# Longer rows for the general, rounded-weight and residual tiles of a two-layer decoder trunk, and one raw weight buffer fewer

## The chip, the cores and the metric

The kernel runs on 1 core of one Trainium2 chip. The metric is the device time of one execution in microseconds; the time before is the median of 3 runs, 2338.2 us (2337.09 to 2348.92).

## The reference

256 tokens of 2048 features go through two layers. Each layer has a token mixer and a channel mixer, and each of these is wrapped in the same way; everything is float32.

```python
mod = c_act @ ada_w[i] + ada_b[i]
sh1, sc1, g1, sh2, sc2, g2 = jnp.split(mod[:, None, :], 6, axis=-1)
h = x * (1.0 + sc1) + sh1
y = fox_attention(h, ...) if i % 2 == 0 else swa_attention(h, ...)
x = layer_norm(ALPHA * x + (1.0 + g1) * y, ln_mix_g[i], ln_mix_b[i])
h = x * (1.0 + sc2) + sh2
y = conv_ffn(h, ffn_w_up[i], ffn_conv_w[i], ffn_conv_b[i], ffn_w_down[i])
x = layer_norm(ALPHA * x + (1.0 + g2) * y, ln_ffn_g[i], ln_ffn_b[i])
```

The mixers are a softmax attention with a forget gate (16 heads of 128) in layer 0 and a sliding-window attention with sinks (32 query heads of 64, 4 key heads) in layer 1. The channel mixer is `(silu(conv(h @ w_up)) gated) @ w_down` with 2 x 5632 hidden features. All weights, about 590 MB of them, are read once.

## The kernel before, in words

**Weights as two halves.** `stream` (L254) takes 512 columns of a weight matrix and goes along its rows two chunks of 128 at a time. For each such pair a raw weight tile `w` (128 x 1024 float32, 512 KB, pool `wp`, 10 buffers) is loaded on the SP queue (L259). ScalarE rounds it into a tile `wh` (L262), and VectorE writes the rest, `w - wh`, into a tile `wl` (L273). Both lie in pool `hl`, 4 buffers for each name, used in turn. The activations are held in the same way as a rounded part and a rest, and every product is three matmuls in the rounded format: rounded by rounded, rounded by rest, rest by rounded. One helper (`mm`, L75) records all matmuls, so they are told apart by their tiles.

**Two forms of product.** In both a matmul has a *moving* operand, whose columns stream through, and a *stationary* one of 128 columns, which is loaded just before (PEld in the profile).

- `w_mm` (L306, `ws` in the profile): the weights are stationary, and 256 columns (tokens) of the modulated input `hH` or `hL` move. One pair of chunks gives 24 matmuls in a row that use one `wh` and one `wl`. It makes q and k of the first attention and the up-projections of both channel mixers: 9984 matmuls in all.
- `x_mm` (L282, `xs`): 128 tokens of the activation are stationary, and 512 columns of `wh` or `wl` move. One pair of chunks gives 12 matmuls, three for each chunk and token block. The stationary tile is `hH`/`hL` (v of the first attention, all inputs of the second, and the last four chunks of the output projections: 1056 matmuls), an attention output `oT` (576) or a gated hidden tile `gT` (2112).

**Where the tiles lie.** Pools are laid one behind the other along each partition: constants (among them `x`, `hH`, `hL`), then `wp`, `hl`, `gp`, `tp`, `sp`. `gp` has 24 general tiles of 2048 bytes (`gtile`, L59: queries, keys, v, probabilities, `oT`, `gT`). The built kernel has these first bytes in a partition:

| tile | before | after |
|---|---|---|
| `hH`, `hL` | 40640, 57024 | the same |
| `w` (10 / 9 buffers, 4096 bytes each) | 92576 and on | 92576 and on |
| `wh` (4 buffers) | 133536, 137632, 141728, 145824 | 129440, 133632, 137824, 142016 |
| `wl` (4 buffers) | 149920, 154016, 158112, 162208 | 146208, 150400, 154592, 158784 |
| first `gp` tile, and the step to the next | 166304, 2048 | 162976, 2144 |

**What sets the order.** Beside the streamed weights other work is spread by hand: the six conditioning vectors per layer (`ada_vector`) read their own 512 KB tiles (`wa`, also from `wp`, also on SP) and are multiplied on VectorE (L388); attention heads, evacuations and norms go on by one stage at each weight pair (`later`, `defer`, `step`). The DMA of a raw tile is issued on SP in program order as soon as the last reader of the buffer's previous tile is done, so a raw tile's load starts when the tile ten before it in `wp` is released. The opening reads the first conditioning vectors through the same pool as `wo` tiles (L508).

Of the kernel before, what the change touches and what calls it, by code (L numbers as in the profile page):

```python
# [11 lines left out]
F32R = mybir.dt.float32r  # L12
# [5 lines left out]
P = 128  # L18
D = 2048
S = 256  # L20
# [16 lines left out]
WB = 512  # L37
UK = 4


@with_exitstack
def hybrid_trunk(ctx: ExitStack, tc: tile.TileContext, a: dict, out: bass.AP):
# [5 lines left out]
    cst = ctx.enter_context(tc.tile_pool(name="cst", bufs=1))  # L48
    wp = ctx.enter_context(tc.tile_pool(name="wp", bufs=10))
    hl = ctx.enter_context(tc.tile_pool(name="hl", bufs=4))  # L50
# [8 lines left out]
    def gtile(name="g"):  # L59
        return gp.tile([P, 2, S], F32R, tag="g", name=name)  # L60

# [15 lines left out]
    def pin(ins, on=True):  # L77
        """Keeps ins behind what its engine has been given so far."""
        if on:
            tc.keep_in_program_order(ins)  # L80

    def split(h, l, src):
        """src (float32) -> h rounded, l the rest; the copy on ScalarE."""
        nc.scalar.copy(h, src)
        nc.vector.tensor_tensor(l, src, f32(h), op=ALU.subtract)  # L85
# [4 lines left out]

# [1 line left out]
    rows0 = ttile("rows0").rearrange("p (a b) -> p a b", b=P)  # L92
# [14 lines left out]
    nc.gpsimd.memset(m0, 0.0)  # L107
    # [:, 0]: previous block (key > query stays); [:, 1]: diagonal block (key <= query stays)
    nc.gpsimd.affine_select(out=m0[:, 0, :], in_=m0[:, 0, :], compare_op=ALU.is_gt, fill=NEG, base=0,
# [34 lines left out]
    def columns():  # L144
        """The vectors that lie along features, as columns."""
        r = ttile("rows").rearrange("p (a b) -> p a b", b=P)
# [26 lines left out]
    def rotary():  # L173
        """Sinks on every partition; sines and cosines of the positions' angles."""
        nc.gpsimd.dma_start(sink, a["swa_sinks"][0].partition_broadcast(P))
# [33 lines left out]

# [1 line left out]
    feeds, post, work = [], [], []  # L211

    def then(fn):
        """fn() behind the products of all weights streamed so far."""
        work.append(fn)
        if len(work) == 1 and not ahead[0]:
            settle()
# [9 lines left out]
    def rest(*items):  # L227
        """Residuals of the next weights."""
        n = 0
        for f in items:  # L230
            if f in residuals:
                residuals[f]()
                n += 1
            elif f in weights:
                n += 1
            if n > 2 - (items[0] not in weights):
                return
# [3 lines left out]
    def defer(gen):  # L241
        """gen goes on by one stage behind each of the next splits of weights."""
        post.append(gen)
# [10 lines left out]
    def stream(wsrc, row0, col, ks, use):  # L254
        """use(kc, h, l) for the weights [(row0 + kc) * P.., col:col+WB] of every two chunks kc, kc + 1."""
        for kc in ks[::2]:
            r0 = (row0 + kc) * P
            w = wtile()
            pin(nc.sync.dma_start(w, wsrc[r0:r0 + 2 * P, col:col + WB].rearrange("(k p) f -> p k f", p=P)), False)  # L259
            h = hl.tile([P, 2, WB], F32R, tag="wh", name="wh")  # L260
            l = hl.tile([P, 2, WB], F32R, tag="wl", name="wl")
            pin(nc.scalar.copy(h, w), False)  # L262
# [19 lines left out]
    def x_mm(ps, kc, h, l, stat, last, first=0, ts=range(NT)):  # L282
        """ps[t] [P tokens, WB] += x[:, chunks kc, kc + 1] @ w"""
        for t in ts:
            for i in range(2):
                xh, xl = stat(kc + i, t)
                mm(ps[t], xh, h[:, i, :], start=kc + i == first)
                mm(ps[t], xh, l[:, i, :])
                mm(ps[t], xl, h[:, i, :], stop=kc + i == last)

    def x_mm_end(ps, stat, nk, n):
        """Products like x_mm's; in the last weights those for the first tokens go before the others."""
        kept = []
# [12 lines left out]
    def w_mm(ps, kc, h, l, last=KC - 1, first=0):  # L306
        """ps[i] [P features, 2, S] += (x[:, chunks kc, kc + 1] @ w).T"""
        for i in range(2):
# [7 lines left out]
    def x_stationary(wsrc, col, k0, nk, stat, end=0):  # L316
        """token-major out[t] [P tokens, WB] = x @ w[:, col:col+WB]"""
        ps = x_banks()
        use = x_mm_end(ps, stat, nk, end) if end else lambda kc, h, l: x_mm(ps, kc, h, l, stat, nk - 1)
        stream(wsrc, k0, col, list(range(nk)), use)  # L320
        return ps

    def w_stationary(wsrc, col):
        """feature-major out: two banks of [P, 2, S] = (x @ w[:, col:col+WB]).T"""
        ps = w_banks()
        stream(wsrc, 0, col, list(range(KC)), lambda kc, h, l: w_mm(ps, kc, h, l))
        return ps

# [1 line left out]
    bg = {"wait": [], "run": [], "n": 0, "at": 0, "gap": 1}  # L330

    def later(gens, lag=1):
        """gens start one after another and go on by one stage at each lag-th step."""
        bg["wait"].extend((g, lag) for g in gens)
# [21 lines left out]

# [1 line left out]
    cols = {}  # L358
    gates = {}
# [67 lines left out]
    def release():  # L427
        """The columns that were kept for the time in which TensorE waits."""
        for s_, _ in held:
# [23 lines left out]

# [1 line left out]
    hH = cst.tile([P, KC, S], F32R, name="hH")  # L455
    hL = cst.tile([P, KC, S], F32R, name="hL")

    def mod_turn(k, n=1):
        """Chunks k, k + 1 of x transposed, in n banks."""
        ps = [bank() for _ in range(n)]  # L460
# [26 lines left out]
    def modulate(G, B, norm):  # L487
        """Hands the modulation of normalised x to the next weights, two chunks for each of them."""
        def feed(k):
# [8 lines left out]
    def opening(plan, proj):  # L498
        """First modulation, by pairs of chunks; between them the products that plan names for each pair."""
        CB = 2 * P  # L500
# [51 lines left out]

# [1 line left out]
    stats = cst.tile([P, NT, D // 512, nc.vector.BN_STATS_DIM], F32, name="stats")  # L554
# [25 lines left out]
    def normalise(d):  # L580
        """x <- (x - mean) / deviation, on ScalarE for the first tokens and on VectorE for the others."""
        for t in range(NT):
# [16 lines left out]
    def affine(name, l):  # L599
        """x <- ALPHA * (x * g + b)"""  # L600
        gb, bb = ln_rows(name, l)
# [13 lines left out]
    def merged(l, v, lng, lnb, ll):  # L615
        """Scale and shift of the modulation behind a layer norm with its own g and b."""
        sh, sc = cols[l, v], cols[l, v + 1]
# [6 lines left out]

# [1 line left out]
    def probs(S_ps, skc=None, nskc=None):  # L626
        """Scores [P queries, 128 | 256 keys] -> softmax."""
        regs = ((0, P), (P, 3 * P))
# [19 lines left out]
    def attend(scores, o_halves, rr, v, sinks=()):  # L648
        """The stages of one head from its scores on."""
        sps = bank("S")  # L650
# [18 lines left out]
    def o_tile(kc):  # L669
        """Where chunk kc of the attention's output goes: the last ones where the input was."""  # L670
        if kc >= KC - 4:
# [30 lines left out]

# [1 line left out]
    def fox(l, j):  # L704
# [5 lines left out]
        for b in range(4):  # L710
            nc.sync.dma_start(bfc[32 * b:32 * b + FH, :], a["fox_b_f"][j:j + 1].rearrange("l h -> h l"))
        # weights of the forget gates, in four groups of partitions of the product
        wf = wp.tile([P, KC, FH], F32, tag="w", name="wf")
# [102 lines left out]
        TC = KC // 2  # L816
        # per pair of chunks: blocks of four heads and the pairs of theirs that are multiplied then
        plan = [[], [(0, 0)], [(0, 1)], [(0, 2)], [(0, 3), (1, 0)], [(1, 1), (1, 2)], [(1, 3), (1, 4)], [(1, 5), (1, 6)], [(1, 7)]]
# [55 lines left out]

# [1 line left out]
    def rope(t, buf, nh):  # L876
        """buf [P, nh, 64], the first 16 of each head turned in place."""
        t1, t2, t3 = (tp.tile([P, SG, HR], F32, tag=n, bufs=1, name=n)[:, :nh, :] for n in ("r1", "r2", "r3"))
# [99 lines left out]

# [1 line left out]
    def conv_ffn(l):  # L980
# [63 lines left out]

# [1 line left out]
    def between(l, v, g, b, name, ll):  # L1046
        """From one layer norm, with g and b in rows g, b of lcol, to the modulated input behind it."""
        ada_need(l, v)
# [49 lines left out]
```

## Time and profile before

| | |
|---|---|
| median of the runs shown | 2338.2 us |
| lowest and highest run | 2337.09, 2348.92 us |
| span of the profiled execution | 2347.5 us |
| mean granted TensorE clock in it | 0.981 |
| read from HBM | 594.2 MB, 254 GB/s over the span |

The profiled execution is known by its span, from its first instruction to its last: 9.3 us above the median and 1.4 us below the highest run. In the profile a matmul's own duration is modelled, and matmuls overlap, so their rate is read from the distance of their starts: from the starts in the timeline, or from a piece of the chain of waits that names a length of time and a count of matmuls.

### The profile page before, as it was taken

How to read it: one execution, taken by the hardware profiler on the slowest of the kernel's cores; microseconds unless marked ns; L12 is line 12 of the kernel's file. 1: busy time of each engine (PE TensorE's matmuls, PEld its weight loads, DVE VectorE, ACT ScalarE, POOL GpSimd, SP SyncE). 2: the span in 40 equal slices, each digit the busy share in tenths (PEclk: the TensorE clock that was granted, in tenths of full speed). 3: DMA queues.
4: the chain of work that ended last, by engine and by line, in shares of the span. 5: the costliest groups of instructions: out<-in, count | busy, mean ns of one | idle time of the engine just before them, and what ended most of it. 6: DMA issues, size and time to landing. Idle time of an engine off the chain costs nothing.

```text
span 2347.5 us, 38862 instructions
## 1 busy us (share of the span) xinstructions
PE 2284.1 (97%) x15189; PEld 2075.5 (88%) x15189; DVE 1801.5 (77%) x2539; ACT 1129.1 (48%) x1677; POOL 38.4 (2%) x75
## 2 busy tenths in 40 slices
PE   6899999999999999999999999999999999999997
PEld 5799988789999888999987777789999988999986
DVE  7778878979887877887877976699877655666665
ACT  1336544445555433555534476635555543455542
POOL 1001000010000000000001000000000000000000
PEclk9899999999999999999998999999999999999999
DMA  9998989968877897887895865586878556666553
GB/s 326 304 339 270 350 313 348 332 214 310 308 248 255 294 302 262 279 291 247 289 308 196 315 209 162 165 306 216 291 258 272 180 192 194 189 189 189 189 194 112
DMA packets 285561, 598.87 MB, mean 255 GB/s; under 512 B 20790, under 2 KB 53816, under 8 KB 285376
## 3 DMA queue, kind: packets, MB, share of 16 engines
q1 hardware_dynamic: 284768, 595.85, 75.6%
q8 instruction: 119, 1.95, 0.3%
q0 software_dynamic: 608, 0.53, 0.1%
q14 instruction: 66, 0.54, 0.1%
HBM read 594.21 MB, written 2.10 MB: 254 GB/s over the span
## 4 chain that ended last, share of the span: by engine, by line
PE 92%; DVE 5%; issue 1%; DMA 1%; ACT 1%; POOL 0%; SPq 0%; DVEq 0%; ACTq 0%; POOLq 0%
PE ws L75 50%; PE xs L75 34%; PE S L75 3%; PE o L75 1%; PE sm L75 1%; DVE wl L273 1%; PE cps L75 1%; PE T L657 1%; DVE oacc L520 1%; DVE acc L388 1%; PE sm L465 1%; ACT wh L262 0%; DMA w<-in_swa_w_in_dram 0%; DMA wo<-in_ada_w_dram 0%; PE lg L75 0%
## 5 line engine op out<-in xcount | busy, mean ns | idle before, releaser
L273 DVE TENSOR_TENSOR wl<-w,wh 128x1024 fp32r<-128x1024 f32 x728 | 888.3, 1221 | 419.8 <-ACT wh L262 402.8
L262 ACT CAST wh<-w 128x1024 fp32r<-128x1024 f32 x728 | 764.3, 1052 | 907.1 <-PE ws L75 333.3
L75 PE MATMUL ws<-hH,wh 128*128 128x256 f32 x3328 | 942.1, 283 | 6.0 <-ACT wh L262 6.0
L75 PE MATMUL ws<-hH,wl 128*128 128x256 f32 x3328 | 933.7, 281 | 3.9 <-DVE wl L273 3.7
L75 PE MATMUL ws<-hL,wh 128*128 128x256 f32 x3328 | 934.6, 281 | 0.2 <-DVE hL L85 0.2
L75 PEld LDWEIGHTS ws<-hH,wh 128*128 128x128 f32 x3328 | 631.9, 190 | 10.0 <-ACT wh L262 6.8
L75 PEld LDWEIGHTS ws<-hH,wl 128*128 128x128 f32 x3328 | 630.6, 190 | 5.1 <-DVE wl L273 5.1
L75 PEld LDWEIGHTS ws<-hL,wh 128*128 128x128 f32 x3328 | 632.0, 190 | 2.7 <-issue 1.9
L75 PE MATMUL xs<-wh,gT 128*128 128x512 f32 x1408 | 437.6, 392 | 0.0
L388 DVE SCALAR_TENSOR_TENSOR acc<-wa,cact,acc 128x1024 f32<-128x1024 f32 x308 | 391.2, 1276 | 0.1
L75 PEld LDWEIGHTS xs<-wh,gT 128*128 128x128 f32 x1408 | 266.5, 189 | 55.3
L75 PE MATMUL xs<-wl,gT 128*128 128x512 f32 x704 | 275.6, 391 | 0.0
L75 PEld LDWEIGHTS xs<-wl,gT 128*128 128x128 f32 x704 | 133.2, 189 | 27.7
L75 PE MATMUL xs<-wh,hH 128*128 128x512 f32 x352 | 144.9, 417 | 0.2 <-ACT hH L475 0.2
L75 PE MATMUL xs<-wl,hH 128*128 128x512 f32 x352 | 142.2, 404 | 2.8 <-DVE wl L273 2.7
L75 PE MATMUL xs<-wh,hL 128*128 128x512 f32 x352 | 142.0, 404 | 0.0
L75 PE MATMUL xs<-wh,oT 128*128 128x512 f32 x384 | 126.3, 399 | 0.0
L987 ACT ACTIVATE u<-ws,ccol 128x256 f32<-128x256 f32 x176 | 96.6, 562 | 58.7 <-PE ws L75 51.4
L988 DVE SCALAR_TENSOR_TENSOR u<-ws,ccol,u 128x255 f32<-128x255 f32 x176 | 82.2, 477 | 20.5 <-ACT u L987 20.5
L75 PEld LDWEIGHTS xs<-wh,oT 128*128 128x128 f32 x384 | 72.7, 190 | 16.1 <-issue 0.2
L75 PEld LDWEIGHTS xs<-wl,hH 128*128 128x128 f32 x352 | 68.0, 193 | 19.6 <-DVE wl L273 4.8
L990 DVE SCALAR_TENSOR_TENSOR u<-ws,ccol,u 128x254 f32<-128x254 f32 x176 | 83.1, 476 | 2.0
(211 smaller groups left out, 1613.3 us busy)
## 6 DMA issues: line engine op xcount, KB each, us to landing
w<-in_ffn_w_up_dram SPq DMA_DIRECT2D x352, 512.0 KB, 4.6
wa<-in_ada_w_dram SPq DMA_DIRECT2D x320, 512.0 KB, 5.2
w<-in_ffn_w_down_dram SPq DMA_DIRECT2D x176, 512.0 KB, 4.4
w<-in_fox_w_in_dram SPq DMA_DIRECT2D x96, 512.0 KB, 6.3
wo<-in_ada_w_dram SPq DMA_DIRECT2D x64, 512.0 KB, 7.0
w<-in_swa_w_in_dram SPq DMA_DIRECT2D x40, 512.0 KB, 5.2
w<-in_fox_w_o_dram SPq DMA_DIRECT2D x32, 512.0 KB, 6.4
w<-in_swa_w_o_dram SPq DMA_DIRECT2D x32, 512.0 KB, 4.7
```

Of the source, the lines that this page charges most:

```text
L75: return nc.tensor.matmul(o, lhsT, rhs, start=start, stop=stop, **kw)
L262: pin(nc.scalar.copy(h, w), False)
L273: pin(nc.vector.tensor_tensor(l, w, f32(h), op=ALU.subtract), False)
L388: pin(nc.vector.scalar_tensor_tensor(ac, wo, cact[:, k:k + 1], ac, op0=ALU.mult, op1=ALU.add), True)
L465: nc.tensor.transpose(o[:, t * P:(t + 1) * P], x[:, t, (k + j) * P:(k + j + 1) * P], ident)
L520: nc.vector.scalar_tensor_tensor(acc[:, v, k % 2, :], w[:, k, :], cact[:, kc:kc + 1], acc[:, v, k % 2, :], op0=ALU.mult, op1=ALU.add)
L657: nc.tensor.transpose(tps[:, b * P:(b + 1) * P], pr[:, b * P:(b + 1) * P], ident)
L987: nc.scalar.activation(u, pf, AF.Identity, bias=cw(CW, f), scale=cw(2, f))
L988: nc.vector.scalar_tensor_tensor(u[:, 1:], pf[:, :S - 1], cw(1, f), u[:, 1:], op0=ALU.mult, op1=ALU.add)
L990: nc.vector.scalar_tensor_tensor(u[:, 2:], pf[:, :S - 2], cw(0, f), u[:, 2:], op0=ALU.mult, op1=ALU.add)
```

## The change

Each row of a `gp` tile and of a `wh` or `wl` tile gets 24 more float32 (96 bytes), which nothing reads or writes: 2144 bytes instead of 2048, and 4192 instead of 4096. The shapes that the code works with stay as they are. `wp` has 9 buffers instead of 10. An unused constant and comments go.

```diff
-UK = 4
+SKEW = 24
...
-    wp = ctx.enter_context(tc.tile_pool(name="wp", bufs=10))
+    wp = ctx.enter_context(tc.tile_pool(name="wp", bufs=9))
...
     def gtile(name="g"):
-        return gp.tile([P, 2, S], F32R, tag="g", name=name)
+        return gp.tile([P, 2 * S + SKEW], F32R, tag="g", name=name)[:, :2 * S].rearrange("p (a s) -> p a s", a=2)
...
-            h = hl.tile([P, 2, WB], F32R, tag="wh", name="wh")
-            l = hl.tile([P, 2, WB], F32R, tag="wl", name="wl")
+            h, l = (hl.tile([P, 2 * WB + SKEW], F32R, tag=n, name=n)[:, :2 * WB].rearrange("p (k f) -> p k f", k=2)
+                    for n in ("wh", "wl"))
```

The number of instructions of each kind on each engine stays the same, but for waits. The instructions of POOL and the loads on SP keep their order. On TensorE the order changes in one place, 17 `xs` matmuls of the first attention's v; on ScalarE and VectorE some 90 listed rows change, nearly all of them beside the heads that run at that place.

## The prediction

> **What bounds the kernel now.** I read the page first: the shares of the engines, the clock and the chain of waits.
>
> ```profile
> PE 2284.1 (97%) x15189; PEld 2075.5 (88%) x15189; DVE 1801.5 (77%) x2539; ACT 1129.1 (48%) x1677; POOL 38.4 (2%) x75
> ...
> PEclk9899999999999999999998999999999999999999
> ...
> PE 92%; DVE 5%; issue 1%; DMA 1%; ACT 1%; POOL 0%; SPq 0%; DVEq 0%; ACTq 0%; POOLq 0%
> PE ws L75 50%; PE xs L75 34%; PE S L75 3%; PE o L75 1%; PE sm L75 1%; DVE wl L273 1%; PE cps L75 1%; PE T L657 1%; DVE oacc L520 1%; DVE acc L388 1%; PE sm L465 1%; ACT wh L262 0%; DMA w<-in_swa_w_in_dram 0%; DMA wo<-in_ada_w_dram 0%; PE lg L75 0%
> ```
>
> TensorE sets the end: 92% of the chain is matmuls, 84% the two products `ws` and `xs`, at nearly the full clock. So what counts is the distance from one matmul's start to the next. The chain in order of time has long pieces with nothing else in them:
>
> ```profile
> 303.99 13.99 PE xs L75 x60
> ...
> 1869.73 130.58 PE xs L75 x576
> 2000.32 224.00 PE ws L75 x1920
> ```
>
> A `ws` matmul (256 columns) takes 224.00 / 1920 = 116.67 ns. An `xs` matmul (512 columns) takes 130.58 / 576 = 226.7 ns in the down-projection, where the stationary tile is `gT`, but 13.99 / 60 = 233.2 ns in the first attention's v, where it is `hH` or `hL`. The clock is the same. Is it the stage or the tile? The output projection uses both kinds of stationary tile one behind the other, so I read TensorE's timeline there (first column: start).
>
> ```profile
> 450.58 0.40 PE L75 MATMUL xs<-wh,hL 128*128 128x512 f32 x1
> 450.81 0.40 PE L75 MATMUL xs<-wh,hH 128*128 128x512 f32 x1
> 451.05 0.40 PE L75 MATMUL xs<-wl,hH 128*128 128x512 f32 x1
> 451.28 0.40 PE L75 MATMUL xs<-wh,hL 128*128 128x512 f32 x1
> 451.52 0.40 PE L75 MATMUL xs<-wh,oT 128*128 128x512 f32 x1
> 451.75 0.39 PE L75 MATMUL xs<-wl,oT 128*128 128x512 f32 x1
> 451.98 0.62 PE L75 MATMUL xs<-wh,oT 128*128 128x512 f32 x2
> 452.44 0.39 PE L75 MATMUL xs<-wl,oT 128*128 128x512 f32 x1
> 452.66 0.62 PE L75 MATMUL xs<-wh,oT 128*128 128x512 f32 x2
> 453.12 0.39 PE L75 MATMUL xs<-wl,oT 128*128 128x512 f32 x1
> ```
>
> Three `hH`/`hL` matmuls take 451.28 - 450.58 = 0.70 us, 233 ns each. Three `oT` matmuls take 452.66 - 451.98 = 0.68 us, 227 ns each, within two matmuls of the change of tile. So it is the stationary tile. What differs is its place: `hH` and `hL` begin at a multiple of 64 bytes; `wh`, `wl`, `oT` and `gT` all begin 32 bytes past one. I call a matmul **level** when its moving and stationary tile lie alike to 64 bytes, and **offset** when they differ by 32. Before, all 2688 `xs` on `oT` and `gT` are level (226.7 ns), and all 1056 `xs` on `hH`/`hL` and all 9984 `ws` are offset. The two offset rates are one: 233.2 ns for 512 columns, 116.67 for 256.
>
> **The change part by part.** The durations are from the profiled execution, whose span of 2347.5 us lies 9.3 above the median of the runs, 2338.2; I take the differences from it and add them to the median.
>
> *Longer rows.* 2144 and 4192 bytes are odd multiples of 32, so every second buffer moves from one class to the other, while `hH` and `hL` stay. I counted the matmuls of the built kernel after the change: of the 2688 `xs` on `gp` tiles, 1356 become offset, with 467 switches between the classes on the way; of the 1056 on `hH`/`hL`, 528 become level; of the 9984 `ws`, 4992 become level, in whole weight tiles of 24 (208 of them).
>
> - `xs` on `gp` tiles: 1356 x (233.2 - 226.7) = +8.8 us. About 234 switches lead back to level, and the first level matmul at 451.52 still took 0.23 us (to 451.75), some 4 ns more than the later ones: +1.0. Sum +9.8. Bounds: +5 if a switch costs nothing and half of it is hidden in the attention stages, +17.5 if no short level stretch ever gets to 226.7 (2688 x 6.5).
> - `xs` on `hH`/`hL`: 528 x -6.5 = -3.4 us. Bounds: -3.4 and 0.
> - `ws` is the open term. No `ws` of before is level. If level and offset stand as 226.7 to 233.2 for 256 columns too, a level `ws` takes 113.4 ns, and 4992 of them give -16.3 us. Against that stand the only level matmuls of 256 columns in the rounded format, the scores of the first attention:
>
> ```profile
> 413.11 0.28 PE L75 MATMUL S<-qh 128*128 128x256 f32 x1
> 413.23 0.28 PE L75 MATMUL S<-ql,qh 128*128 128x256 f32 x1
> 413.35 0.28 PE L75 MATMUL S<-qh,ql 128*128 128x256 f32 x1
> 413.47 0.22 PE L75 MATMUL S<-mask,identr 128*128 128x128 f32 x1
> 413.52 0.44 PE L75 MATMUL xs<-wh,oT 128*128 128x512 f32 x1
> 413.81 0.39 PE L75 MATMUL xs<-wl,oT 128*128 128x512 f32 x1
> 414.04 0.63 PE L75 MATMUL xs<-wh,oT 128*128 128x512 f32 x2
> 414.51 0.39 PE L75 MATMUL xs<-wl,oT 128*128 128x512 f32 x1
> 414.73 0.63 PE L75 MATMUL xs<-wh,oT 128*128 128x512 f32 x2
> 415.20 0.39 PE L75 MATMUL xs<-wl,oT 128*128 128x512 f32 x1
> 415.43 0.62 PE L75 MATMUL xs<-wh,oT 128*128 128x512 f32 x2
> 415.89 0.39 PE L75 MATMUL xs<-wl,oT 128*128 128x512 f32 x1
> 416.12 0.39 PE L75 MATMUL xs<-wh,oT 128*128 128x512 f32 x1
> ```
>
> The three take 413.47 - 413.11 = 0.36 us, 120 ns each: no gain. But they are only three in a row, just behind an interruption, and the same rows show that the level `xs` behind it need time too: from 413.81 to 415.89, nine take 2.08 us, 231 ns each, before the next takes 0.23. So a level stream must first settle, some 10 matmuls after an interruption and two after a mere change of tile. The value I take lies between: of the 24 level `ws` of a weight tile the first 10 stay at 116.7 and 14 run at 113.4, so 208 x 14 x -3.3 ns = -9.6 us. Bounds: downwards, a `ws` can't come faster than weight loads follow each other. Transposes with a moving operand of 128 columns, each with a load of its own, come thus in the chain:
>
> ```profile
> 347.86 0.33 PE T L657 x3
> ```
>
> That is 110 ns each, so at most 4992 x -6.7 = -33 us. Upwards, the scores' 120 ns on 4992: +16.6 us.
>
> A rule of the Trainium skill speaks against any such effect. The page "TensorE: Matmul & The Clock Gate", Part 2, under "Step-by-step: what each phase is for", gives TensorE two independent read ports and says: "Loading the next tile's weights doesn't steal SBUF read bandwidth from the running matmul." By that a stationary tile's address could not change the rate, and the sum would be the raw buffer's alone. The rows at 451 us disagree, 233 against 227 ns for the same form.
>
> *One raw buffer fewer.* A raw tile's load is now issued when the tile nine before it is released. The 512 KB loads on SP pass in this many:
>
> ```profile
> w<-in_ffn_w_up_dram SPq DMA_DIRECT2D x352, 512.0 KB, 4.6
> wa<-in_ada_w_dram SPq DMA_DIRECT2D x320, 512.0 KB, 5.2
> w<-in_ffn_w_down_dram SPq DMA_DIRECT2D x176, 512.0 KB, 4.4
> w<-in_fox_w_in_dram SPq DMA_DIRECT2D x96, 512.0 KB, 6.3
> wo<-in_ada_w_dram SPq DMA_DIRECT2D x64, 512.0 KB, 7.0
> ...
> 455.75 4.03 DMA w<-in_fox_w_o_dram
> 1327.99 7.77 DMA w<-in_swa_w_in_dram
> ```
>
> These rows alone are 1008 loads in 2347.5 us, one in about 2.3 us, so each load is issued about 2.3 us later. Nine buffers behind each other are 9 x 2.3 = 21 us, and a load lands in 4.4 to 7.0: in the projections the cover is wide, and the term is nothing. Where loads are late already, at 455.75 and 1327.99 in the chain, the delay comes through: up to 2 x 2.3 us. I take +2. Bounds 0 and +8 (the opening, full of loads as it is, adding as much again). If the cover were gone, every load would wait.
>
> *The rest.* ScalarE's rounding and VectorE's subtraction write to other offsets; I cost that at nothing, since both engines have room (48% and 77% busy) beside TensorE. If their spans grew by a tenth, VectorE would still be under 90%. The moved rows on TensorE, ScalarE and VectorE are the same work within one block of heads: nothing, give or take 2 us.
>
> Sum: 9.8 - 3.4 - 9.6 + 2 = -1.2 us, so 2337.0 us.
>
> **The rivals.**
>
> - *Slower: the streams never settle.* `gp` tiles change class every few matmuls, `wh` and `wl` with every weight tile. If a settled state needs a longer run than that, all level `xs` take the 231 ns of the rows behind 413.81, offset ones 233.2, and level `ws` the 118 between 116.7 and the scores' 120. On `gp` tiles 1332 x 4.3 + 1356 x 6.5 = +14.5; on `hH`/`hL` 528 x -2.2 = -1.2; `ws` 4992 x 1.3 = +6.5; loads +2. That is +21.8: 2360 us. It decides as soon as a level `ws` takes 116.7 ns or more: then the sum is at least 9.8 - 3.4 + 2 = +8.4, 2346.6. For it: the scores' rows. Against it: the rows at 451 us, where two matmuls were enough, and that 256 columns show the same offset rate as 512.
> - *Faster: level `ws` settle at once, or bytes beyond 64 count too.* Two of 24 matmuls lost: 208 x 22 x -3.3 = -15.1; with 9.8 - 3.4 and no cost of loads -8.7: 2329.5. After the change there are also distances of 64 and 96 bytes to 128, which no row of before shows; with the bound of -33 for `ws` it is 2338.2 + 9.8 - 3.4 - 33 = 2311.6.
> - *Nothing happens to the rates*, as the skill's rule has it. As a mechanism of this kernel: the 6.5 ns come from something else about `hH`, say that rounded part and rest lie 16 KB apart and in `gT` 1 KB. Then only the loads remain, +2: 2340 us. Against it: the offset rate is the same for two different pairs of tiles.
>
> **How the numbers follow.** Forecast (2330 to 2346): 0.36. Never settling (2346 to 2366): 0.34, spread over its span, as the point of decision lies at its near end. Faster (2311 to 2330): 0.20. Nothing (2338 to 2342): 0.10. The likeliest single time is that where the level gain and the `gp` loss nearly cancel, so 2337, its own range 2330 to 2346. The range reaches into both other cases, to the middle of the faster one and to the far end of the slower: 2319 to 2366. A measurement of this kernel can tell about 0.5%, 11.7 us, from no change: faster means under 2326.5, slower over 2349.9. Of the faster case 0.17 lies under, with 0.03 more from the forecast's own lower bounds (+5 on `gp`): 0.20. Of never settling 0.27 lies beyond, with 0.08 more from the `gp` bound of +17.5 and late loads: 0.35. The same: 0.45.
>
> **What would show it.** In the chain of the changed kernel, the long `ws` piece near 2000 us should take under 224.00 us for 1920: 219 by the forecast, 217 if it settles at once, 224 to 229 if it never does. The `gT` piece of 576 should take over 130.58: 132.5 to 133.5. A timeline in the up-projection should show groups of 24 at 116.7 in turn with groups that begin so and end near 113.4. In v of the first attention tiles of 12 `xs` should alternate between 233 and 227. If `xs` on `gp` tiles stays at 226.7 throughout, the rule of 64 bytes is wrong; if late loads in the chain grow past 5 us in all, the buffer was worth more.

## The result and the profile after

The changed kernel takes 2375.03 us (median of 4 runs, 2372.61 to 2379.33), the kernel before beside it 2343.56 (2337.09 to 2352.29). The ratio is 1.0139, with a 95% interval of 1.0106 to 1.0172: slower by 25 to 40 us. The span of its profiled execution is 2377.6 us, 30.1 over that of before.

The shares of the engines on the page of the changed kernel, and its chain of waits by engine:

```profile
PE 2316.6 (97%) x15189; PEld 2094.9 (88%) x15189; DVE 1804.3 (76%) x2539; ACT 1126.6 (47%) x1677; POOL 38.4 (2%) x75
...
PE 92%; DVE 4%; DMA 1%; issue 1%; ACT 1%; POOL 0%; SPq 0%; DVEq 0%; POOLq 0%; ACTq 0%
```

TensorE is busy 32.5 us longer with the same number of instructions; VectorE and ScalarE are within 3 us. So the time went into the matmuls. In the chain in order of time (start, length, what, how many) the same three pieces as before, with the loads that the chain has now:

```profile
195.04 4.87 DMA w<-in_fox_w_in_dram
...
304.43 13.95 PE xs L75 x60
...
465.91 4.60 DMA w<-in_fox_w_o_dram
...
1325.31 4.84 DMA w<-in_swa_w_in_dram
...
1891.01 133.72 PE xs L75 x576
2024.73 227.19 PE ws L75 x1920
```

A `ws` takes 227.19 / 1920 = 118.33 ns (before 116.67), an `xs` on `gT` 133.72 / 576 = 232.2 (before 226.7), an `xs` on `hH`/`hL` 13.95 / 60 = 232.5 (before 233.2). Times their numbers: 9984 x 1.66 = +16.6, 2688 x 5.45 = +14.7, 1056 x -0.7 = -0.7 us, +30.6 together. The late loads are at other places: 4.87 + 4.60 + 4.84 = 14.3 us, where the two quoted of before took 11.8. They grew by 2.5 us, not past the 5 at which the prediction would have put more on the buffer.

Do the four weight buffers differ? TensorE's timeline in the second up-projection shows it, if only the first matmul of each weight tile is kept:

```profile
2109.79 0.28 PE L75 MATMUL ws<-hH,wh 128*128 128x256 f32 x1
...
2112.53 0.28 PE L75 MATMUL ws<-hH,wh 128*128 128x256 f32 x1
...
2115.45 0.28 PE L75 MATMUL ws<-hH,wh 128*128 128x256 f32 x1
...
2118.29 0.28 PE L75 MATMUL ws<-hH,wh 128*128 128x256 f32 x1
...
2121.15 0.28 PE L75 MATMUL ws<-hH,wh 128*128 128x256 f32 x1
```

The four tiles take 2.74, 2.92, 2.84 and 2.86 us, 114, 122, 118 and 119 ns for each of 24 matmuls. Which buffer each tile has is known from the built kernel: the second, third, first and fourth. The second and the fourth are level; so they are not alike, and the third, offset like the first, is slower than the `ws` of before. Only the second does much what the forecast said of both level ones: over the whole run its first four matmuls take 117.4 ns and the others 113.4.

### The profile page after: what moved, and what is told of

Its sections match the earlier page's. It is cut to its first block, busy times and chain, and to the rows that moved or that the text cites. A ratio compares the mean times of both kernels' runs of the same rounds, so it can differ in the third digit from the quotient of the medians.

```text
span 2377.6 us, 38848 instructions
## 1 busy us (share of the span) xinstructions
PE 2316.6 (97%) x15189; PEld 2094.9 (88%) x15189; DVE 1804.3 (76%) x2539; ACT 1126.6 (47%) x1677; POOL 38.4 (2%) x75
## 4 chain that ended last, share of the span: by engine, by line
PE 92%; DVE 4%; DMA 1%; issue 1%; ACT 1%; POOL 0%; SPq 0%; DVEq 0%; POOLq 0%; ACTq 0%
PE ws L75 50%; PE xs L75 34%; PE S L75 3%; PE o L75 1%; PE sm L75 1%; PE cps L75 1%; DVE wl L273 1%; DVE acc L388 1%; PE T L657 1%; DVE oacc L520 1%; PE sm L465 1%; ACT wh L262 0%; DMA wo<-in_ada_w_dram 0%; DVE x L565 0%; DVE t L563 0%
## 5 line engine op out<-in xcount | busy, mean ns | idle before, releaser
L75 PE MATMUL xs<-wh,gT 128*128 128x512 f32 x1408 | 444.6, 396 | 0.0
```

What stands on the lines that cost most here:

```text
L75: return nc.tensor.matmul(o, lhsT, rhs, start=start, stop=stop, **kw)
```

## The experiments

**Theory.** A matmul's rate hangs on the distance of its two tiles, the moving one's first byte less the stationary one's, in steps of 32 bytes, and the change replaced two lucky distances by all of them. **Rivals.** The raw buffer; that streams with changing distances never settle, so that only mixing costs; that the place of a single tile counts, or something else about `hH`.

In the diffs, `ph`, `pm` and `pg` are pools with one unused tile each, ahead of `wh`, between `wh` and `wl`, and ahead of the `gp` tiles; a "distance" is counted modulo 256 or 512 bytes. Numbers that were constants at the head of a kernel are written out. "Over all starts" means the mean from one start to the next over a whole run, with each matmul's distance from the built kernel and the breaks in the stream left out. Time after a colon is the median with the ratio to the kernel before beside it and its interval.

### The two parts of the change, and the buffer alone

```diff
-    wp = ctx.enter_context(tc.tile_pool(name="wp", bufs=10))
+    wp = ctx.enter_context(tc.tile_pool(name="wp", bufs=9))
```

> Rows as before, only one raw weight buffer fewer (9). Theory (the matmul rates make the difference, through where their tiles lie): ws 116.7 ns and xs on gT 226.7 ns as before, time within 3 us of before (2343 to 2347 where before is 2343.6). Rival (the raw buffer makes it): some 31 us slower as the changed kernel, about 2375, with TensorE waiting for loads at many places.

Measured: 2346.99 us, 1.0016 (1.0006 to 1.0026), so +3.7 us. The chain has the rates of before to the digit:

```profile
1864.86 130.58 PE xs L77 x576
1995.43 224.00 PE ws L77 x1920
```

The buffer is about a ninth of the loss (1 to 6 us by the interval); the rest is the rows'.

```diff
-            h = hl.tile([P, 2, WB], F32R, tag="wh", name="wh")
-            l = hl.tile([P, 2, WB], F32R, tag="wl", name="wl")
+            h, l = (hl.tile([P, 2 * WB + 24], F32R, tag=n, name=n)[:, :2 * WB].rearrange("p (k f) -> p k f", k=2)
+                    for n in ("wh", "wl"))
```

> Longer rows for wh and wl alone (4192 bytes), gp tiles as before, 9 raw buffers. Theory (each rate hangs on the distance of the two tiles): ws as in the changed kernel, 118.3 ns, xs on gT slower than 226.7 too, since the moving wh and wl now lie at four distances from it, but with fewer switches (one for each 12 matmuls): 228 to 232. Sum 9984 x 1.6 + 2688 x 1.3 to 5.3 = +19 to +30 us. Rival (gT's own place makes xs slow): xs on gT stays 226.7, sum +16.

Measured: 2376.44 us, 1.0146 (1.0129 to 1.0162), +34 us, of which the buffer 3.7.

```profile
1891.39 133.60 PE xs L77 x576
2024.99 227.23 PE ws L77 x1920
```

`ws` 118.3 ns and `xs` on `gT` 231.9, both as in the changed kernel, though the `gp` tiles lie as before among themselves. The rival that `gT`'s own place makes `xs` slow falls. This half of the change is already the whole loss.

```diff
-        return gp.tile([P, 2, S], F32R, tag="g", name=name)
+        return gp.tile([P, 2 * S + 24], F32R, tag="g", name=name)[:, :2 * S].rearrange("p (a s) -> p a s", a=2)
```

> Longer rows for gp tiles alone (2144 bytes), wh and wl as before, 9 raw buffers. Theory: ws stays 116.7, xs on hH stays 233.2, xs on gp tiles about 232 as in the changed kernel: +14 us. Rival (the place of wh and wl sets all rates): nothing, 0 to +2 us.

Measured: 2360.63 us, 1.0077 (1.0062 to 1.0092), +18 us, 14 beside the buffer's 3.7, as the theory has it.

```profile
1871.85 133.68 PE xs L77 x576
2005.53 224.00 PE ws L77 x1920
```

`ws` is untouched, `xs` on `gT` 232.1 ns. So the two halves don't add up: for `xs` either one spreads the distances over all, and a second spreading changes nothing.

### Rows longer by 128 bytes

The same as the change, with 32 more float32 in each row instead of 24.

> Longer rows for all three by 128 bytes instead of 96, 9 raw buffers, so that all tiles lie at many offsets, but each pair keeps its distance modulo 128. Theory (only the distance modulo 128, or 64, counts): rates as before, 116.7 and 226.7, time as with nine buffers alone. Rival (any change of offset from matmul to matmul keeps the streams from settling, or distances modulo 256 and 512 count): 10 to 30 us slower.

Measured: 2366.98 us, 1.0098 (1.0084 to 1.0113), +23 us. So the distance modulo 64 or 128 does not decide: `xs` on `gT` takes 133.16 / 576 = 231.2 ns.

```profile
1881.73 133.16 PE xs L77 x576
2014.89 224.75 PE ws L77 x1920
```

Over all starts, by distance modulo 512: `ws` takes 116.7 ns at 32 and at 288, 117.6 and 117.7 at 160 and 416; `xs` on `gp` tiles 230.1 and 230.3 at 0 and 256, 232.9 and 232.6 at 128 and 384. So 256 bytes bring a rate back, and 128 don't.

### One distance for all: the table of steady rates

Rows as before, 10 buffers, and unused bytes ahead of the pools, so that each kind of matmul keeps one distance throughout:

```diff
+    ph = ctx.enter_context(tc.tile_pool(name="ph", bufs=1))
     hl = ctx.enter_context(tc.tile_pool(name="hl", bufs=4))
+    pg = ctx.enter_context(tc.tile_pool(name="pg", bufs=1))
...
+    for pool, n in ((ph, PAD_H), (pg, PAD_G)):
+        if n:
+            nc.gpsimd.memset(pool.tile([P, n], F32, name="pad"), 0.0)
```

`PAD_H` and `PAD_G` are 8 and 8, then 16 and 16, 24 and 0, 40 and 24, 48 and 40, 56 and 0 float32.

> Rows as before, 10 raw buffers; 32 unused bytes ahead of wh and wl and 32 more ahead of the gp tiles. Every kind of matmul keeps one distance (moving minus stationary, modulo 512) throughout: ws 256 (before 288), xs on gp tiles 480 (before 0), xs on hH/hL 256 (before 224). Theory (each distance has its own steady rate): ws about 119 ns, as the weight tiles at 0 and 128 showed in the changed kernel, so 9984 x 2.2 = +22 us; xs on gp tiles 233 as offset ones, +17: about 2380. Rival (only mixing costs, and level ws are at least as fast): ws 113.4 to 116.7, xs on gp tiles 233: 2328 to 2361.

> As the run with 32 and 32 bytes, but 64 and 64: ws at distance 224, xs on gp tiles at 448, xs on hH/hL at 288. Theory (each distance has its own steady rate): ws 122.5 ns as the wl tiles at 224 showed, 9984 x 5.8 = +58 us; xs on gp tiles 226.7 to 231 (level), 0 to +12: 2390 to 2415. Rival (only mixing costs): ws 116.7, xs on gp tiles 226.7, no change: 2344.

> As before, with 10 raw buffers, but 96 unused bytes ahead of wh and wl, so that ws has distance 192 throughout, xs on gp tiles 0 as before, xs on hH/hL 320. Theory (each distance has its own steady rate): ws 113.5 to 114 ns, as the second of the four buffers showed in the changed kernel, 9984 x -2.7 to -3.2 = -27 to -32 us; xs on hH/hL 230, -3: 2309 to 2314. Rival (the good rate of that buffer came from its neighbours, or only mixing costs): ws 116.7, 2344.

> As before, with 10 raw buffers; 160 unused bytes ahead of wh and wl and 96 more ahead of the gp tiles: ws at distance 128, xs on gp tiles at 416, xs on hH/hL at 384. Theory (each distance has its own steady rate): ws 119.5 ns, +28 us; xs on gp tiles 233, +17: about 2388. Rival (only mixing costs): ws 113.4 to 116.7, xs on gp tiles 233: 2328 to 2361.

> As before, with 10 raw buffers; 192 unused bytes ahead of wh and wl, 160 more ahead of the gp tiles. Modulo 256: ws at distance 96, xs on gp tiles at 96, xs on hH/hL at 160. It fills the table of steady rates. Theory (steady rate for each distance, repeating after 256 bytes): xs on hH/hL 234.2 ns as on gp tiles at 416 (the same modulo 256); ws 118 to 120 as the buffer at 96 showed in the changed kernel; xs on gp tiles over 227: 2355 to 2395. Rival (hH and gp tiles differ in themselves): xs on hH/hL not at 234.

> As before, with 10 raw buffers, but 224 unused bytes ahead of wh and wl: ws at distance 64 throughout, xs on gp tiles 0 as before, xs on hH/hL 192. Theory (steady rate for each distance): ws 114 to 116 ns, as the wl tiles at 320 (64 modulo 256) had 115.4 in the changed kernel, -7 to -27 us; xs on hH/hL 233.3 as on gp tiles at 448: 2316 to 2336. Rival (level distances all alike, as the prediction had it): 115.9 as at 192, 2327.

Measured, in this order: 2388.76 us, 1.0199 (1.0176 to 1.0222); 2373.75, 1.0138 (1.0113 to 1.0164); 2326.74, 0.9939 (0.9915 to 0.9963); 2383.47, 1.0179 (1.0156 to 1.0202); 2393.52, 1.0213 (1.0198 to 1.0229); 2356.6, 1.0051 (1.0037 to 1.0066).

The chains show each run's three rates, v of the first attention (60), `gT` (576) and `ws` (1920). With 8 and 8:

```profile
303.35 13.64 PE xs L77 x60
...
1894.25 134.39 PE xs L77 x576
2028.64 230.38 PE ws L77 x1920
```

With 16 and 16:

```profile
300.21 13.98 PE xs L77 x60
...
1883.20 134.40 PE xs L77 x576
2017.60 227.20 PE ws L77 x1920
```

With 24 and 0:

```profile
295.73 13.75 PE xs L77 x60
...
693.24 76.17 PE ws L77 x672
...
1847.71 130.57 PE xs L77 x576
1978.28 226.13 PE ws L77 x1920
```

With 40 and 24:

```profile
303.07 13.94 PE xs L77 x60
...
713.09 79.74 PE ws L77 x672
...
1894.84 134.94 PE xs L77 x576
2029.78 230.40 PE ws L77 x1920
```

With 48 and 40:

```profile
303.40 14.05 PE xs L77 x60
...
1899.87 134.39 PE xs L77 x576
2034.26 230.41 PE ws L77 x1920
```

With 56 and 0:

```profile
298.31 13.99 PE xs L77 x60
...
1870.24 130.59 PE xs L77 x576
2000.83 226.13 PE ws L77 x1920
```

Length by count gives the table, in ns (before's own distances in bold; `ws` at 160 is not from a run of its own but from the one with 128 bytes, 2 x 224.75 / 1920 - 116.67):

| distance modulo 256 | 0 | 32 | 64 | 96 | 128 | 160 | 192 | 224 |
|---|---|---|---|---|---|---|---|---|
| `ws` | 120.0 | **116.7** | 117.8 | 120.0 | 118.7 or 120.0 | 117.4 | 113.3 or 117.8 | 118.3 |
| `xs` on `hH`/`hL` | 227.3 | 233.0 | 229.2 | | 232.3 | 234.2 | 233.2 | **233.2** |
| `xs` on `gp` tiles | **226.7** | | | 233.3 | | 234.3 | 233.3 | 233.3 |

What follows:

- Rates above 116.7 and 226.7 stand in runs without any mixing. The rival that only mixing costs falls.
- `hH` at distance 0 runs like `gT` there (227.3 and 226.7), and both agree at 160, 192 and 224. So it isn't something else about `hH`, and the rival by which nothing could change falls.
- 0, 64, 128 and 192 are all level, and have 120.0, 117.8, 118.7 or 120.0, and 113.3 or 117.8 for `ws`, 227 to 233 for `xs`. Level and offset are no classes.
- `xs` before had the best of its distances, and `ws` the second best. The mean of a row is what a spread over all distances should cost if nothing else counted: `ws` (192 as 117.8, 128 as 120.0) 118.5, `xs` (empty places from the other row) 231.9. The changed kernel has 118.3 and 232.2. By single weight tiles it agrees less well: the four above, with `wh` and `wl` at 192 and 64, 96 and 224, 32 and 160, 0 and 128, should take 117.8, 119.4, 116.9 and 120.0 ns (two thirds of the matmuls use `wh`), and took 114, 122, 118 and 119.
- Several expectations missed: with 56 and 0 the sign too (2316 to 2336 expected), with 16 and 16 (2390 to 2415) and 24 and 0 (2309 to 2314) the size. From the changed kernel's groups I took 122.5 for 224, 114 for 192 and 115.4 for 64; alone these have 118.3, 115.9 over all starts, and 117.8. At 192 there are two rates: 76.17 / 672 = 113.3 ns in one up-projection, 226.13 / 1920 = 117.8 in another, with the same buffers. The time of that run, 15.5 us under the kernel beside it, has both in it. In both runs with two rates (24 and 0, 40 and 24), a stretch without breaks keeps its rate from about the tenth matmul to its end. The stretches of 120, 1152 and 1920, which follow `xs` without a pause, have the slower one (at 128, 120.0), and the other long ones the faster, but for one of 1796 at 192. What sets it is not shown.

### Everything moved alike

```diff
+    nc.gpsimd.memset(cst.tile([P, 8], F32, name="pad"), 0.0)
```

ahead of the first constant.

> As before, with 10 raw buffers, but 32 unused bytes ahead of the first constant, so that every tile of SBUF begins 32 bytes later and no distance between two tiles changes. Theory (only the distance of moving and stationary tile counts): all rates as before, ws 116.7, xs on gp tiles 226.7, on hH/hL 233.2, 2343. Rival (where a tile itself lies to 64 bytes counts): rates move as they do with distances, ws by up to 3 ns, 2310 to 2390.

Measured: 2342.36 us, 0.9996 (0.9983 to 1.0009). `xs` x576 in 130.58 us, `ws` x1920 in 224.00, as before. The distances decide, not the places: a common shift by 32 bytes changes nothing, and the rival of a tile's own place falls.

### Distances that change from weight tile to weight tile

The kernel with longer rows for `wh` and `wl` alone and 9 raw buffers, and between them

```diff
+    for pool, n in ((pm, 32),):
+        nc.gpsimd.memset(pool.tile([P, n], F32, name="pad"), 0.0)
```

so that `wh` and `wl` of one weight tile lie alike.

> Longer rows (4192 bytes) for wh and wl alone, 9 raw buffers, as in the run with those alone, but 128 unused bytes between the wh and the wl tiles, so that wh and wl of one weight tile lie alike modulo 512 and the distance changes only from weight tile to weight tile. Modulo 256, ws has 0, 32, 96, 192 in turn. Theory (steady rates, averaged): ws at 0 119.9, at 32 116.7, at 192 115.9 ns, at 96 what the run with 192 and 160 bytes shows, mean 117.5 to 118; xs on gp tiles (at 64, 128, 160, 224) 229.6, 232.4, 234.2, 233.3, mean 232.4: +9 + 15 - 2 and the buffer's 3.6, 2369. Rival (changing from tile to tile is what costs): ws not the mean of the steady rates in any group, 118.3 and more.

Measured: 2377.17 us, 1.0139 (1.0118 to 1.016), 8 us over what the steady rates were expected to give. By distance, over all starts: `ws` at 0, 32, 96 and 192 takes 119.5, 116.7, 119.8 and 117.4 ns, the steady rates to 0.5 (192 between its two). That the expected mean was too low lies mostly at 96 and 192, of which the one was not known then, and the other taken as 115.9. So changing the distance every 24 matmuls adds nothing to the steady rates that shows here, except at 192: nearly all weight tiles there have the slower rate, which the run with 24 and 0 has in part of its stretches only.

### wh and wl 128 bytes apart

In the changed kernel `wh` and `wl` of a weight tile also lie 128 bytes apart, modulo 256, and its groups differ from the table: 114 ns for wh at 192 with wl at 64. These runs give every weight tile one such group, with constant distances: 96 bytes ahead of `wh` (in the first alone), 128 between `wh` and `wl`, 128 ahead of the `gp` tiles.

> Rows as before, 10 raw buffers; 96 unused bytes ahead of wh, 128 between wh and wl, 128 more ahead of the gp tiles. In every weight tile ws on wh has distance 192 and ws on wl 64, as in the one group of the changed kernel that ran at 114.2 and 115.3 ns; xs on gp tiles has 0 with wh and 128 with wl. Theory (the neighbour's distance counts too): ws as in that group, mean 114.6, 9984 x -2.2 = -22 us; xs on gp tiles 228.8, +5: 2327 or a little under. Rival (each matmul has the steady rate of its own distance, whatever its neighbours): ws (2 x 115.9 + 117.7) / 3 = 116.5, -3; xs on gp tiles (2 x 227.0 + 232.4) / 3 = 228.8, +5; xs on hH/hL (2 x 229.6 + 233.4) / 3, -2: 2343.

> Rows and wh as before, 10 raw buffers; 128 unused bytes between wh and wl, 128 more ahead of the gp tiles: ws on wh at distance 32, on wl at 160, as in the first group of the changed kernel, which ran at 117.7 and 120.1 ns. Theory (the neighbour's distance counts too): ws mean 118.5, +17 us; xs on gp tiles +5: 2365. Rival (own distance alone): ws (2 x 116.8 + 117.7) / 3 = 117.1, +4; xs on gp tiles +5: 2352.

Measured: 2326.46 us, 0.9918 (0.9904 to 0.9932), and 2374.7, 1.0118 (1.0102 to 1.0134). The first one's chain:

```profile
697.42 76.21 PE ws L79 x672
...
1845.27 134.39 PE xs L79 x576
1979.66 217.65 PE ws L79 x1920
```

Now `ws` takes 113.4 ns in both pieces, and over all starts 113.6 at 192 and at 64 alike. Alone, 64 had 117.8, and 192 had 113.3 only in part of its stretches. And `xs` on `gT` takes 233.3 throughout, though two of three matmuls have distance 0: over all starts even those take 232.5. The other run's chain:

```profile
1885.87 134.39 PE xs L79 x576
2020.26 228.25 PE ws L79 x1920
```

Here `ws` takes 228.25 / 1920 = 118.9, where the distances alone would give (2 x 116.7 + 117.4) / 3 = 116.9, and `xs` on `gT` 233.3 too. So a neighbour's distance counts, in both directions. Theory and rival both missed `xs`: they put it at 228.8. That the first run came out at the expected 2327 is luck: `ws` was faster than expected by 9984 x 1.2 = 12 us, and `xs` slower by 2688 x 4.5 = 12. In the second run (2365 expected) nothing made up for `xs`.

### Apart for ws, alike for xs

```diff
-            l = hl.tile([P, 2, WB], F32R, tag="wl", name="wl")
+            at = (32 * apart + 32 * (0, 3, 1, 2)[turn[0] % 4]) % 64
+            turn[0] += 1
+            l = lp.tile([P, 2 * WB + 32], F32R, tag="wl", name="wl")[:, at:at + 2 * WB].rearrange("p (k f) -> p k f", k=2)
```

with `apart` true for the weights of `w_mm`, 96 bytes ahead of `wh`, and 10 raw buffers. (The list undoes the 128 bytes by which the buffers shift, in the order in which the pool hands them out.)

> 10 raw buffers, 96 unused bytes ahead of wh; wl rows are 128 bytes longer, and where in its row a wl begins is chosen by its use: for ws at distance 64 while its wh is at 192, for xs at the same distance as its wh (0 on gp tiles, 64 on hH/hL). Theory (a matmul's rate hangs on its own distance and on those of the matmuls beside it): ws 113.6 ns as where wh and wl lie 128 bytes apart, xs on gp tiles 227.0 as where all three lie alike, on hH/hL 229.6: 9984 x -3.2 - 1056 x 3.5 = -36 us, 2308 where before is 2344. Rival (the slow xs of that run came from something else, such as the gp tiles' new place): xs on gp tiles stays near 233, 2324.

Measured: 2311.46 us, 0.9856 (0.983 to 0.9881).

```profile
362.57 13.75 PE xs L79 x60
...
693.62 76.21 PE ws L79 x672
...
1838.28 130.57 PE xs L79 x576
1968.86 217.63 PE ws L79 x1920
```

`ws` 113.4, `xs` on `gT` 226.7, on `hH`/`hL` 229.2: all three as expected, and the time within 4 us. With `wl` back at its distance, `xs` is back; the `gp` tiles' place was not it. It is faster than both kernels, 33 us under the one before, by the same kind of edit that cost 31.

## Why the prediction was wrong, point by point

The forecast of 2337.0 missed, and the range, whose high end was 2366, did not hold 2375. Against the kernel before beside it, -1.2 us was forecast and +31.5 measured.

- **What bounds it**: right. Nearly all of the loss is in the time from one matmul's start to the next, and the reading at 451 us, that the rate changes with the stationary tile, stands.
- **The rule of 64 bytes, level and offset**: here it failed. Before shows two distances, 0 and 32 modulo 256 (224 where the operands are exchanged), and I took them for two classes. The table has eight places of 32 bytes, the only steps tried, and repeats after 256, and among level places `ws` differs by up to 6.7 ns, `xs` by 6.6. Both loss terms were worked out from the two classes.
- **`ws`, -9.6 us**: the term that carries the miss. It measured +16.6. Half of the `ws` were expected to go from 116.7 to 113.4; instead all of them together, spread over eight distances, have a mean of 118.3. That 116.67 is half of 233.3 let me carry the gain of a level `xs` over to `ws`, and it does not carry over: at distance 0, `xs` is at its best and `ws` at its worst. The scores' rows, 120 ns for three matmuls at distance 0, agree with the steady 120.0 of that distance, and I had weighed them down as "three in a row". The bound that they gave, +16.6, meets the measured value by luck: it has half of the `ws` at 120.0 and the rest at 116.7, and the run has tiles from 114 to 122.
- **Streams settle**: this reading stands, some 10 matmuls after a break. Over all starts of the kernel before, `xs` on `gp` tiles take 231.9 ns for the first three after a break and 226.7 from the thirteenth; in the last experiment `ws` go from 117.1 to 113.3. What a stream settles to is the rate of its distances, which can be slower too: at distance 0 `ws` go from 118.3 to 120.0, so a break is not what made the scores slow.
- **`xs` on `gp` tiles, +9.8**: right in sign, and in that the distance costs, measured +14.7. It was mis-sized since of the eight distances only 0 and 64 are cheap, not every second one.
- **`xs` on `hH`/`hL`, -3.4**: about -0.7, from the pieces of v, for the same reason.
- **The raw buffer, +2**: +3.7 alone, within its bounds of 0 and +8.
- **Moved rows and the other engines, nothing**: nothing speaks against it. VectorE and ScalarE are within 3 us, and the sum leaves no loss over; the moved rows had no run of their own.
- **The sum**: 16.6 + 14.7 - 0.7 + 3.7 = +34.3 against 31.5 by the medians and 25 to 40 by the interval.
- **The slower rival** had the decisive point right, that with a level `ws` at 116.7 or more the kernel is slower, and its `ws` piece (224 to 229) holds 227.19. Its mechanism, streams that never settle, isn't needed for the loss, as the mean of the steady rates gives it. Yet neighbours count, as the runs with `wh` and `wl` apart show; in the changed kernel what they give and take cancels nearly: -3.6, +2.3, +1.4 and -0.8 ns for the four weight tiles above.
- **The rule of the Trainium skill**, in "TensorE: Matmul & The Clock Gate", Part 2, that loading the next weights takes nothing from the running matmul: by it the stationary tile's place would not count. These runs disagree with that. The same 512-column matmul on the same data takes 226.7 to 234.3 ns by the distances of its tiles, and the 256-column one 113.3 to 120.0. Whether it is the load's read that delays the matmul, no run shows.

What stays open: why. That the two reads meet in the same part of the memory fits a period of 256 bytes, the neighbours and the two rates at 192; it is argued from these, and no run shows it.

## What to carry to other kernels

Before giving tiles "many offsets", look what rate the present offsets have: a spread buys the mean of all distances, and a regular layout can be tuned to the best one by a few unused bytes. Two values in a profile are not a rule for all others; a handful of runs with one constant shift each gives the table, as long as neighbouring matmuls keep one distance too, and the best layout found was worth 1.4% here. A short, odd row that contradicts the rule (the three scores) deserves its full weight in the sum.

## What the hardware showed that was not expected

- In this rounded float32 format the rate of back-to-back matmuls depends on the distance of moving and stationary tile in SBUF (steps of 32 bytes), repeating after 256: 113.3 to 120.0 ns for 256 columns and 226.7 to 234.3 for 512, with the granted clock at 1.00 in the long pieces. A common shift of all tiles by 32 bytes changes nothing (0.9996).
- One and the same distance can have two lasting rates: at 192, 113.3 ns (672 in 76.17 us) and 117.8 (1920 in 226.13 us); at 128, 118.7 (672 in 79.74 us) and 120.0 (1920 in 230.40 us).
- The distance of the matmul beside it counts: two of three `xs` at distance 0 run at 232.5 ns when the third is at 128, and at 226.7 when all three are at 0.
